# Folded attention: part of the output is stored in two unfinished parts, q's rotation reads the matmul banks, and the softmax scaling is one operation

## The chip, the core and the metric

The kernel runs on one core of one Trainium2 chip. A core has five engines that work side by side, each through its own queue and in the order of that queue: TensorE (PE in the profile; PEld is its weight load), VectorE (DVE), ScalarE (ACT), GpSimd (POOL) and SyncE (SP, which here issues most DMAs). They meet through semaphores. SBUF is the on-chip memory of 128 partitions, PSUM holds the matmul results in banks of 128 x 512 fp32, and HBM lies outside. The metric is the device time of one execution in microseconds (us); lower is better.

## What is computed

One layer of a hybrid decoder on x of 1024 x 1024 fp32: a norm, one projection into nine parts, retention (branch A), sliding-window attention with sinks (branch B), gates, and a SwiGLU feed-forward. The change touches branch B:

```python
aq = rotary(aq.reshape(B, S, ATTN_Q_HEADS, ATTN_HEAD_DIM), pos)   # 16 heads of 64
...
scores = jnp.einsum('bnqhgd,bnkhd->bnhgqk', qb, kb) * (d ** -0.5)
scores = jnp.where(mask, scores, -1e30)                           # window of 128
m = jnp.maximum(jnp.max(scores, axis=-1, keepdims=True), sink)
e = jnp.exp(scores - m)
probs = e / (jnp.sum(e, axis=-1, keepdims=True) + jnp.exp(sink - m))
out = jnp.einsum('bnhgqk,bnkhd->bnqhgd', probs, vb)
branch_b = ay.reshape(B, S, ATTN_Q) @ w_attn_out[l]
```

where rotary makes `x1*cos - x2*sin` and `x2*cos + x1*sin` from the two halves of a head.

## The kernel before

**Numbers in two parts.** Matmul operands are split into a high part (rounded to the matmul's format, called hi, `wh`, `ph`) and the rest (lo, `wl`, `pl`), and each product is three matmuls: hi x hi, hi x lo, lo x hi. ACT makes a high part (a cast), DVE the low part (a subtraction). `split` (L131) does this for weights; their tiles `wh` and `wl` have two buffers each.

**q, in quads.** `quad_q(g)` (L403) makes the rotated q of the four heads of group g. Its weights arrive as two raw slabs and are split into two pairs of tiles, one for the first halves of the heads (z = 0), one for the second (z = 1). Four groups of 24 matmuls follow, each into one of three banks tagged `acc`, in the order (z, half) = (0,0), (0,1), (1,0), (1,1), where half is a half of the 1024 positions. After each, ACT copies the bank out with the bias (L427). When both z of a half are there, DVE and ACT turn them (L437 to L446): four multiplications by cos and sin, a subtraction and an addition, and two splits. The result `stg` (one buffer, shared with k's staging) is stored to HBM as 1 MB (`q_d`, L448) and loaded back in another layout (L450).

**Attention, in 32 units.** A unit is one of four groups of heads (g) and one of eight blocks of 128 positions (b). `u_scores` (L462) makes the scores of four heads into two banks; ACT copies one part, DVE puts the masked other part in (L483) and takes the minimum (the scores are negated), with the sink in an extra column that POOL writes (L469); ACT makes the exponentials (L493), DVE the reciprocal of their sum, and ACT scales each of the four heads (L498). In block 0 one DVE operation per head (L490) masks and takes the minimum. A window of two blocks of keys is folded into one block of 128 columns, since of each pair of keys only one is inside the window. `u_transpose` (L500) turns the probabilities on TensorE (`pT`), splits them, and by a mask makes `qh`, `ql` for the difference of v's two blocks; `u_values` (L520) multiplies with v into one bank `pv`. In that bank two heads share each pair of quarters, and its rows of the two halves have to be added across: ACT copies them (L529, L530), DVE adds (L531, L532), ACT and DVE split the sum (L534, L535) into hi and lo, which overwrite q. After four blocks SP stores the result, 1 MB, to `ay_d` (L568).

**What sets the order.** quad_q(0) runs alone. Then a generator `Fill` supplies other matmuls between the pieces of the units: quad_q(1) to (3) and the gate projections `g6`, ... (`dense_g`, L178, in two groups of 24 each, evicted by ACT with a tanh). In a step i, TensorE's program has the transposes of unit i-1, the scores of unit i, some 7 to 8 steps of three fill matmuls, and the values of unit i-1 (L555 to L574). A scheduler then orders each engine's queue by priorities; weights are pulled ahead (`high_priority`). Half-way the v weights `wv` are loaded into a buffer that the q of groups 0 and 1 has left, and later pairwise subtracted (L578).

**The column pairs.** Ten pairs of column blocks (`w*`, from L783 on) of the projection follow, in seven products each (P1 to P7, Strassen's scheme), with operands split three products ahead by `wprep_to` (ACT hi, DVE lo, POOL the sums of weights). Here DVE, ACT and POOL work in the order in which the code is written (`in_order`, L903). Results of pairs 0, 2, 4 and 6 are rotated: r lies in a tile tagged `rr` (three buffers), SP copies its halves crosswise to `xw`, then POOL and DVE multiply (`turn`, L839) and DVE adds and SP stores to `rk_d` (`total`, L843), two and three products later. At pair 2 the attention output of groups 0 and 1 comes back into `ay` (`load_ay(0)`, L891), to be used after the column pairs; at the end of them that of groups 2 and 3.

## Time and profile before

| what | value |
|---|---|
| median of 3 runs | 1569.12 us (1568.94 to 1569.2) |
| the profiled execution: its time / its span | 1566.55 us / 1564.8 us |
| mean granted TensorE clock | 0.998 |
| attention stage, first q matmul to first v matmul | 42.1 to 351.0 us |
| v projection | 351 to 427 us |
| column pairs | 427 to 620 us |
| DMA traffic | 228.43 MB, 146 GB/s on the mean |

The profile is of one execution. A busy time is the sum of an engine's instructions; "idle before, <-releaser" is the time an engine stood still ahead of a group of instructions and what ended it; in the table of waits a row reads: engine, what waited, for whom, us in total, times, longest. Names like `aq`, `pT`, `stg` are tiles of the program, and L-numbers its lines. A matmul's record is longer (0.39 us) than the distance to the next one, since they overlap in the array; the pace is read from the starts. PEld rows are loads of weights for the next matmul and run beside the current one.

### The profile page before, as it was taken

The page shows a single profiled execution, that of the slowest core. Times are in us where ns is not written, and L with a number is a line of the kernel's source. Part 1 is how long each engine was busy: PE and PEld are TensorE (multiplying, and loading weights), DVE is VectorE, ACT ScalarE, POOL GpSimd, SP SyncE. Part 2 cuts the span into 40 slices and gives each one's busy share as a digit, 9 for nine tenths or more (in the row PEclk, how much of TensorE's full clock was granted, in tenths as well). Part 3 has the DMA queues.
Part 4 walks back from the last instruction along what each step waited for, and adds up shares of the span by engine and source line. Part 5 has one row for each costly group of instructions (what it writes and reads, how often), then busy time and mean ns, then how long its engine had stood idle before and what let it go on. Part 6 is the DMA issues. An engine that isn't in the chain of part 4 may idle for free.

```text
span 1564.8 us, 20561 instructions
## 1 busy us (share of the span) xinstructions
PE 1549.0 (99%) x7323; PEld 1284.4 (82%) x7323; DVE 1016.2 (65%) x1668; ACT 735.2 (47%) x1556; POOL 375.3 (24%) x320
## 2 busy tenths in 40 slices
PE   9999999999999999999999999999999999999998
PEld 8887777788888888888888888888888888888886
DVE  6559878677667663877557789444444444678756
ACT  6358878834233333544224366333333333444445
POOL 2000000000055441000021124655555555100001
PEclk9999999999999999999999999999999999999999
DMA  6554655340464455654565402333333333862233
GB/s 219 168 160 123 208 209 162 129 134 35 154 204 149 138 165 189 227 193 150 175 195 190 167 1 88 121 102 102 108 103 109 105 101 102 289 255 90 92 102 127
DMA packets 152581, 228.43 MB, mean 146 GB/s; under 512 B 9307, under 2 KB 81821, under 8 KB 150942
## 3 DMA queue, kind: packets, MB, share of 16 engines
q1 hardware_dynamic: 152476, 227.10, 44.4%
q8 instruction: 58, 0.95, 0.2%
q14 instruction: 45, 0.37, 0.1%
q10 hardware_dynamic: 2, 0.00, 0.0%
HBM read 152.36 MB, written 69.99 MB: 142 GB/s over the span
## 4 chain that ended last, share of the span: by engine, by line
PE 88%; ACT 6%; DVE 4%; issue 1%; DMA 1%; SPq 0%; POOL 0%; POOLq 0%; ACTq 0%; DVEq 0%
PE fA L1545 15%; PE fB L1545 8%; PE dA L1847 7%; PE wA L869 7%; PE dxP L1847 6%; PE fC L1545 4%; PE wB L869 3%; PE wo L1379 3%; PE va L714 3%; PE woP L1379 2%; PE vP L714 2%; PE acc_ba L161 2%; PE acc_ba L159 2%; PE acc_ba L160 2%; PE acc_bb L159 2%; PE acc_bb L160 2%
## 5 line engine op out<-in xcount | busy, mean ns | idle before, releaser
L1847 PE MATMUL dA<-dwP,daP 128*128 128x512 f32 x528 | 120.6, 389 | 0.0
L1847 PEld LDWEIGHTS dA<-dwP,daP 128*128 128x128 f32 x528 | 99.0, 188 | 20.7 <-DVE dwP L135 0.2
L1847 PE MATMUL dxP<-dwP,daP 128*128 128x512 f32 x396 | 90.2, 389 | 0.0
L1847 PEld LDWEIGHTS dxP<-dwP,daP 128*128 128x128 f32 x396 | 74.3, 188 | 15.4
L159 PE MATMUL acc_g<-h,wh_g 128*128 128x512 f32 x192 | 76.9, 401 | 0.6 <-ACT wh_g L132 0.6
L469 POOL COPY sc<-nsink 128x4 f32<-128x4 f32 x32 | 11.2, 349 | 273.6 <-PE pT L505 237.2
L160 PE MATMUL acc_g<-h,wh_g 128*128 128x512 f32 x192 | 76.4, 398 | 0.0
L161 PE MATMUL acc_g<-h,wl_g 128*128 128x512 f32 x192 | 76.4, 399 | 0.0
L1620 POOL TENSOR_TENSOR xf<-xf 128x512 f32<-128x512 f32 x40 | 61.6, 1541 | 30.4 <-issue 28.8
L1551 POOL TENSOR_TENSOR xf<-xf 128x512 f32<-128x512 f32 x33 | 47.3, 1435 | 58.5 <-ACT xf L1553 26.9
L493 ACT ACTIVATE sc<-sc,nm 128x129 f32<-128x129 f32 x128 | 50.4, 397 | 19.3 <-DVE nm L485 15.4
L135 DVE TENSOR_TENSOR dwP<-wd,dwP 128x512 fp32r<-128x512 f32 x77 | 52.7, 684 | 4.6 <-ACT dwP L132 4.6
L1752 POOL TENSOR_TENSOR rs_f<-tot,mhalf 128x1 f32<-128x1 f32 x8 | 4.8, 606 | 205.4 <-DVE tot L1749 205.4
L132 ACT CAST daP<-daP 128x512 fp32r<-128x512 f32 x42 | 26.0, 621 | 55.0 <-PE dxP L1847 26.7
L132 ACT CAST dwP<-wd 128x512 fp32r<-128x512 f32 x77 | 47.4, 616 | 8.8 <-PE dA L1847 6.6
L159 PE MATMUL acc_bb<-ay,wh_bb 128*128 128x512 f32 x128 | 51.2, 400 | 0.0
L160 PE MATMUL aq<-h,wh_aq 128*128 128x512 f32 x128 | 50.6, 395 | 0.0
L161 PE MATMUL aq<-h,wl_aq 128*128 128x512 f32 x128 | 50.5, 395 | 0.0
L159 PE MATMUL aq<-h,wh_aq 128*128 128x512 f32 x128 | 50.3, 393 | 0.0
L160 PE MATMUL acc_bb<-ay,wh_bb 128*128 128x512 f32 x128 | 50.3, 393 | 0.0
L161 PE MATMUL acc_bb<-ay,wl_bb 128*128 128x512 f32 x128 | 50.1, 391 | 0.0
L159 PE MATMUL acc_ba<-yg,wh_ba 128*128 128x512 f32 x128 | 49.9, 390 | 0.0
(840 smaller groups left out, 4350.1 us busy)
## 6 DMA issues: line engine op xcount, KB each, us to landing
act_d<-xf SPq DMA_DIRECT2D x77, 256.0 KB, 2.0
daP<-act_d SPq DMA_DIRECT2D x21, 512.0 KB, 3.5
q_d<-stg SPq DMA_DIRECT2D x8, 1024.0 KB
q<-q_d SPq DMA_DIRECT2D x32, 256.0 KB, 6.0
ay_d<-q SPq DMA_DIRECT2D x8, 1024.0 KB
ay<-ay_d SPq DMA_DIRECT2D x4, 2048.0 KB, 14.3
wr_daP<-act_d SPq DMA_DIRECT2D x14, 512.0 KB, 6.8
wr_g<-in_w_in SPq DMA_DIRECT2D x12, 512.0 KB, 4.2
```

What stands on the lines that cost most here:

```text
L132: nc.scalar.copy(hi, raw)
L135: return nc.vector.tensor_tensor(out=lo, in0=raw, in1=f32(hi), op=ALU.subtract)
L159: nc.tensor.matmul(pt, hi[:, k, :], xh, start=(k == 0), stop=False)
L160: nc.tensor.matmul(pt, hi[:, k, :], xl, start=False, stop=False)
L161: nc.tensor.matmul(pt, lo[:, k, :], xh, start=False, stop=(k == 7))
L493: nc.scalar.activation(sc[:, j, 0:P + 1], sc[:, j, 0:P + 1], AF.Exp, scale=-1.0, bias=nm[:, j:j + 1], accum_out=den[:, j:j + 1])
L714: nc.tensor.matmul(vbanks[pr][tt], x_[:, c], w[:, u, :], start=(fresh and k + z == 0), stop=(k == 3 and z == 2), skip_group_check=not fresh)
L869: nc.tensor.matmul(pt, o[:, w, k, :], v, start=(first and k + z == 0), stop=(k == 3 and z == 2), skip_group_check=not first)
L1379: nc.tensor.matmul(bank, v[:, q + u, k, c], w[y][:, k % 2, :], start=(first and z == 0), stop=(last and z == 2), skip_group_check=not tracked)
L1545: nc.tensor.matmul(pt, o[:, w, k, :], v, start=(first and n == 0), stop=(n == 11), skip_group_check=not first)
L1620: nc.gpsimd.tensor_tensor(out=o, in0=a, in1=b, op=op)
L1847: nc.tensor.matmul(banks[tt], a[:, u, c], w[:, v, :], start=(fresh and f + z == 0), stop=(f == NP - 1 and z == 2), skip_group_check=not fresh)
```

## The change

1. In groups 0 and 1, `u_values` no longer adds, splits and overwrites q: ACT copies the bank as it is to a tile `xy` (two buffers), and POOL issues a DMA of 256 KB per unit to a new HBM tile `xy_d`. The four stores to `ay_d` of these groups go. Groups 2 and 3 are as before.
2. `load_ay(0)` brings the two parts to the places of hi and lo in `ay` (eight DMAs of 512 KB). `split_ay`, called after product P3 of the pairs 4, 5, 6 and 7, adds the two, and makes hi (ACT) and lo (DVE), two halves each time, with a scratch tile `ays` from the tag `rr`.
3. `quad_q` runs its groups as (half, z) = (0,0), (0,1), (1,0), (1,1). ACT's copy with the bias goes; DVE multiplies straight from the bank, adding the bias in the same operation (`scalar_tensor_tensor`), twice per bank. The tiles `ra` and `rb` go, and k's and v's staging take the tags `ph`, `qh` and `ql`.
4. The scaling by the reciprocal is one DVE operation on four heads in groups 0 and 1, and on two heads in groups 2 and 3, where ACT still scales the other two.

```diff
...
     mb_d = dram.tile([8, P, S], F32, name="mb_d")
     ay_d = dram.tile([4, P, 4, S], F32, name="ay_d")
+    xy_d = dram.tile([2, P, 4, S], F32, name="xy_d")
     v_d = dram.tile([P, NB, D], F32, name="v_d")
     rk_d = dram.tile([8, P, S], F32, name="rk_d")
...
         def ak_evac(half, pt):
             c = slice(half * 512, half * 512 + 512)
-            xb = r512("ra", 2, f"kxb{half}")
+            xb = r512(("ph", "qh")[half], 1, f"kxb{half}")
             nc.scalar.activation(xb, pt, AF.Identity, bias=akb, scale=-0.125)
             stg = w1.tile([P, 4, 512], F32, tag="stg", bufs=1, name=f"kstg{half}")
...
 
         def av_evac(half, pt):
-            vt = r512("rb", 1, f"vt{half}")
+            vt = r512("ql", 1, f"vt{half}")
             nc.scalar.activation(vt, pt, AF.Identity, bias=bcol[:, 33:34], scale=1.0)
             p2 = ps("t", 2, f"vT{half}")
...
                     nc.vector.tensor_tensor(out=lo, in0=rv_[:, :, z], in1=f32(hi), op=ALU.subtract)
             hp.__exit__(None, None, None)
-            ab = {}
-            for z, half in ((0, 0), (0, 1), (1, 0), (1, 1)):
+            for half, z in ((0, 0), (0, 1), (1, 0), (1, 1)):
                 pt = acc(f"aq{g}{z}{half}")
                 yield from mm_g(pt, w[z], H, half * 512)
-                t = r512("ra" if z == 0 else "rb", 2 - z, f"q{g}{z}{half}")
-                nc.scalar.activation(t, pt, AF.Identity, bias=bcol[:, QB + 4 * z + g:QB + 4 * z + g + 1], scale=1.0)
-                ab[z, half] = t
+                c = slice(half * 512, half * 512 + 512)
+                if z == 0:
+                    stg = w1.tile([P, 4, 512], F32, tag="stg", bufs=1, name=f"stg{g}{half}")
+                    s0, s1, s2, s3 = (stg[:, i, :] for i in range(4))
+                bias = bcol[:, QB + 4 * z + g:QB + 4 * z + g + 1]
+                for o, tab in (((s2, 0), (s0, 1)), ((s1, 1), (s3, 0)))[z]:
+                    nc.vector.scalar_tensor_tensor(out=o, in0=pt, scalar=bias, in1=atab[:, tab, c], op0=ALU.add,
+                                                   op1=ALU.mult)
                 if z == 0:
                     yield
                     continue
-                c = slice(half * 512, half * 512 + 512)
-                a, b = ab[0, half], t
-                stg = w1.tile([P, 4, 512], F32, tag="stg", bufs=1, name=f"stg{g}{half}")
-                s0, s1, s2, s3 = (stg[:, i, :] for i in range(4))
-                cos, sin = atab[:, 0, c], atab[:, 1, c]
-                nc.vector.tensor_tensor(out=s2, in0=a, in1=cos, op=ALU.mult)
-                nc.vector.tensor_tensor(out=s1, in0=b, in1=sin, op=ALU.mult)
                 nc.vector.tensor_tensor(out=s2, in0=s2, in1=s1, op=ALU.subtract)
-                nc.vector.tensor_tensor(out=s0, in0=a, in1=sin, op=ALU.mult)
-                nc.vector.tensor_tensor(out=s3, in0=b, in1=cos, op=ALU.mult)
                 nc.vector.tensor_tensor(out=s3, in0=s3, in1=s0, op=ALU.add)
                 nc.scalar.activation(s0.bitcast(F32R), s2, AF.Copy)
...
             rd = tiny.tile([P, 4], F32, tag="rd", name=f"rd{g}{b}")
             nc.vector.reciprocal(rd, den)
-            for j in range(4):
+            nd = 4 if g < 2 else 2
+            nc.vector.tensor_tensor(out=sc[:, 0:nd, 0:P], in0=sc[:, 0:nd, 0:P],
+                                    in1=rd[:, 0:nd].rearrange("p (j o) -> p j o", o=1).to_broadcast([P, nd, P]),
+                                    op=ALU.mult)
+            for j in range(nd, 4):
                 nc.scalar.activation(sc[:, j, 0:P], sc[:, j, 0:P], AF.Copy, scale=rd[:, j:j + 1])
 
...
                 for z, p in enumerate(hl):
                     nc.tensor.matmul(pv, vb[:, g // 2, :], p, start=(n + z == 0), stop=(n == len(parts) - 1 and z == 1))
+            if g < 2:
+                t = w1.tile([P, 512], F32, tag="xy", bufs=2, name=f"xy{g}{b}")
+                nc.scalar.copy(t, pv)
+                nc.gpsimd.dma_start(xy_d[g, :, :, qc], t.rearrange("p (j q) -> p j q", j=4))
+                return
             pvv = pv.rearrange("p (i z q) -> p i z q", i=2, z=2)
             tm = w1.tile([P, 2, P], F32, tag="tm", bufs=1, name=f"tm{g}{b}")
...
                     g, b, _, Bt, jb, _ = geo(i - 1)
                     c = slice((b // 4) * 512, (b // 4) * 512 + 512)
-                    nc.sync.dma_start(ay_d[g, :, :, c], f32(Bt[:, jb:jb + 4, c]))
+                    if g > 1:
+                        nc.sync.dma_start(ay_d[g, :, :, c], f32(Bt[:, jb:jb + 4, c]))
             if i == 2 * NB + 4:
                 wv = act.tile([P, 16, 512], F32, tag="B", name="wv")
...
         AY.append(act.tile([P, 8, 1024], F32R, tag="B", name=f"ay{z}"))
         for g in range(2):
-            nc.sync.dma_start(f32(AY[z][:, 4 * g:4 * g + 4, :]), ay_d[2 * z + g])
+            if z:
+                nc.sync.dma_start(f32(AY[z][:, 4 * g:4 * g + 4, :]), ay_d[2 * z + g])
+                continue
+            for r in range(2):
+                for u in range(2):
+                    nc.sync.dma_start(f32(AY[z][r * 64:r * 64 + 64, 4 * g + u:4 * g + u + 3:2, :]),
+                                      xy_d[g, u * 64:u * 64 + 64, r:r + 3:2, :])
+
+    def split_ay(k):
+        for q in range(2):
+            c = slice(q * 512, q * 512 + 512)
+            hi, lo = AY[0][:, 2 * k, c], AY[0][:, 2 * k + 1, c]
+            t = wtile("rr", 3, f"ays{k}{q}")
+            nc.vector.tensor_tensor(out=t, in0=f32(hi), in1=f32(lo), op=ALU.add)
+            nc.scalar.copy(hi, t)
+            nc.vector.tensor_tensor(out=lo, in0=t, in1=f32(hi), op=ALU.subtract)
 
     qTs, kTs, kts, rgs = {}, {}, {}, {}
...
             if (j, pr) == (2, "P1"):
                 load_ay(0)
+            elif j in (4, 5, 6, 7) and pr == "P3":
+                split_ay(j - 4)
             elif (j, pr) == (8, "P5"):
                 load_kq(0, 0)
```

How this moves instructions, at three places. Lines after L63 are shifted by 1 to 23 in the changed kernel.

First, DVE's queue in the first quad. `stg_739` is the rotation of quad 0's first half, `q_683` and `q_737` the copies of its two banks, `wl_aq_799` and `wl_aq_801` the low parts of quad 1's weights (z = 0 and z = 1). Before:

```order
L420 TENSOR_TENSOR wl_aq_799<-wr_aq_802,wh_aq_798 128x512
L336 TENSOR_TENSOR kstg_607<-kxb_605,kstg_607 128x512
L420 TENSOR_TENSOR wl_aq_799<-wr_aq_808,wh_aq_798 128x512
L437 TENSOR_TENSOR stg_739<-q_683,atab 128x512
L438 TENSOR_TENSOR stg_739<-q_737,atab 128x512
L440 TENSOR_TENSOR stg_739<-q_683,atab 128x512
L439 TENSOR_TENSOR stg_739<-stg_739 128x512
L441 TENSOR_TENSOR stg_739<-q_737,atab 128x512
L442 TENSOR_TENSOR stg_739<-stg_739 128x512
```

In the changed kernel the rotation is `stg_684`, the banks are `aq_659` and `aq_687` (quad 0's first and second group), and quad 1's weights for z = 0 are `wl_aq_792` with the high part `wh_aq_791`:

```order
L337 TENSOR_TENSOR kstg_608<-kxb_606,kstg_608 128x512
L421 TENSOR_TENSOR wl_aq_792<-wr_aq_795,wh_aq_791 128x512
L421 TENSOR_TENSOR wl_aq_792<-wr_aq_801,wh_aq_791 128x512
L432 SCALAR_TENSOR_TENSOR stg_684<-aq_659,bcol,atab 128x512 x2
L432 SCALAR_TENSOR_TENSOR stg_684<-aq_687,bcol,atab 128x512 x2
L437 TENSOR_TENSOR stg_684<-stg_684 128x512
L438 TENSOR_TENSOR stg_684<-stg_684 128x512
```

The first operations that read a bank stand behind quad 1's weight subtractions, whose buffer (that of quad 0's z = 0 weights) is read until the third group. The fourth group writes the bank of `aq_659` again.

Second, TensorE's queue at quad 1's end, where `s_890` and `s_899` are the scores of unit 0, `s_946` and `s_956` those of unit 1, and `aq_873` and `aq_926` quad 1's third and fourth group. Before, all four groups of quad 1 and two of the gate's stood ahead of the scores:

```order
L161 MATMUL acc_g_1_1163<-h_111,wl_g_1024 128x512
L159 MATMUL acc_g_1_1163<-h_111,wh_g_1023 128x512
L477 MATMUL s_885<-kst,q_641 128x128 [waits DMAHW5_49,DMAHW6_49,DMAHW4_49,DMAHW7_49,DMAHW2_49,DMAHW0_49]
L478 MATMUL s_885<-kst,q_641 128x128
L477 MATMUL s_885<-kst,q_641 128x128
```

After, the scores come between the third and the fourth group, which waits for DVE:

```order
L162 MATMUL aq_873<-h_112,wl_aq_792 128x512
L473 MATMUL s_890<-kst,q_642 128x128 [waits DMAHW5_49,DMAHW6_49,DMAHW4_49,DMAHW7_49,DMAHW2_49,DMAHW0_49]
...
L473 MATMUL s_946<-kst,q_642 128x256 [waits DVE_49]
L474 MATMUL s_946<-kst,q_642 128x256
L473 MATMUL s_946<-kst,q_642 128x256
L474 MATMUL s_946<-kst,q_642 128x256
L473 MATMUL s_956<-kst,q_642 128x256 [waits DVE_49]
L474 MATMUL s_956<-kst,q_642 128x256
L473 MATMUL s_956<-kst,q_642 128x256
L474 MATMUL s_956<-kst,q_642 128x256
L160 MATMUL aq_926<-h_111,wh_aq_793 128x512 [waits DVE_49]
```

and in DVE's queue the reads of `aq_807`, the bank that `aq_926` writes, stand behind the gate's weights and unit 0's four minima (`nm_888`):

```order
L136 TENSOR_TENSOR wl_g_1003<-wr_g_1000,wh_g_1002 128x1024
L486 ISA sc_886,nm_888<-s_890,amask,nsink 128x128
L486 ISA nm_888 128x1
L486 ISA sc_886,nm_888<-s_890,amask,nsink 128x128
L486 ISA nm_888 128x1
L486 ISA sc_886,nm_888<-s_899,amask,nsink 128x128
L486 ISA nm_888 128x1
L486 ISA sc_886,nm_888<-s_899,amask,nsink 128x128
L486 ISA nm_888 128x1
L432 SCALAR_TENSOR_TENSOR stg_832<-aq_807,bcol,atab 128x512 x2
```

Third, DVE's queue in the column pairs, after product P3 of pair 4. `r_5020` and `r_4863` are the same result before and after, `w5P_5098` and `w5P_4949` the weights of product P5 of pair 5. Before:

```order
L834 SCALAR_TENSOR_TENSOR r_5091<-wB_4988,bcol,u_4983 128x512
L844 TENSOR_TENSOR r_5020<-r_5020,xw_5022 128x512
L135 TENSOR_TENSOR w5P_5098<-wr_wp_4886,w5P_5098 128x512
L849 TENSOR_TENSOR r_5114<-wC_5101,p_5047 128x512
L841 TENSOR_TENSOR r_5069<-r_5069,rtabkT 128x512
```

After (the waits are printed with the rows):

```order
L840 SCALAR_TENSOR_TENSOR r_4934<-wB_4831,bcol,u_4826 128x512 [waits DMAHW0_49,DVE_49,PE_49]
L850 TENSOR_TENSOR r_4863<-r_4863,xw_4865 128x512 [waits DVE_49,Pool_49]
L913 TENSOR_TENSOR ays_4941<-ay_4440 128x512 [waits DMAHW6_49,DVE_49]
L915 TENSOR_TENSOR ay_4440<-ays_4941,ay_4440 128x512 [waits Activation_49]
L913 TENSOR_TENSOR ays_4945<-ay_4440 128x512 [waits DVE_49]
L915 TENSOR_TENSOR ay_4440<-ays_4945,ay_4440 128x512 [waits Activation_49]
L136 TENSOR_TENSOR w5P_4949<-wr_wp_4729,w5P_4949 128x512 [waits Activation_49]
L855 TENSOR_TENSOR r_4965<-wC_4952,p_4890 128x512 [waits DMAHW1_49,PE_49]
```

On ACT the two copies L914 stand in the same way ahead of the high part of `w5P_4949`. After P3 of pair 6 the rows are the same with pair 7's weights.

## The prediction

> **What bounds the kernel now.** I read the busy times first, then the chain that ended last, then the busy time by stage.

> ```profile
> PE 1549.0 (99%) x7323; PEld 1284.4 (82%) x7323; DVE 1016.2 (65%) x1668; ACT 735.2 (47%) x1556; POOL 375.3 (24%) x320
> PE 88%; ACT 6%; DVE 4%; issue 1%; DMA 1%; SPq 0%; POOL 0%; POOLq 0%; ACTq 0%; DVEq 0%
> 106.00:142.00 36.00, 35.87 (x186) 28.65 (x184) 32.30 (x74) 32.45 (x110) 2.80 (x6) 1.00 0.64 187
> 427.00:620.00 193.00, 192.62 (x853) 158.84 (x852) 114.90 (x133) 74.67 (x127) 81.35 (x56) 1.00 0.52 168
> ```

> TensorE is the bound: 88% of the chain is PE. Both kernels issue the same matmuls, so only the time in which PE waits can change. In the rows of stages the columns are the stretch, its length, the busy us of PE, weight loads, DVE, ACT and POOL, the clock, the DMA share and GB/s. In the attention stage ACT and DVE are at 32 of 36 us, as loaded as they get; in the column pairs DVE has 78 us free, ACT 118, and PE loses 0.4 us. So the attention stage has something to win and the column pairs have only something to lose.

> How much can be won? The stage runs from the first q matmul to the first v matmul.

> ```profile
> 42.11 0.40 PE L159 MATMUL aq<-h,wh_aq 128*128 128x512 f32 x1
> ...
> 57.23 0.39 PE L160 MATMUL aq<-h,wh_aq 128*128 128x512 f32 x1
> ...
> 59.95 0.39 PE L160 MATMUL aq<-h,wh_aq 128*128 128x512 f32 x1
> ...
> 95.37 0.28 PE L478 MATMUL s<-kst,q 128*128 128x128 f32 x1
> 95.48 0.27 PE L477 MATMUL s<-kst,q 128*128 128x128 f32 x1
> ...
> 96.82 0.28 PE L478 MATMUL s<-kst,q 128*128 128x256 f32 x1
> 96.94 0.28 PE L477 MATMUL s<-kst,q 128*128 128x256 f32 x1
> ...
> 350.99 0.62 PE L714 MATMUL va<-vP,h 128*128 128x512 f32 x2
> ```

> Starts follow each other at 0.2267 us for 512 columns (2.72 us for 12), 0.11 for 128, 0.12 for 256. The stage has 40 groups of 24 (16 of q, 24 of the gates) and 120 value matmuls of 512 columns: 1080 x 0.2267 = 244.8 us. The scores add 32 x 0.11 + 224 x 0.12 = 30.4, the transposes 128 x 0.11 = 14.1: 289.3 us. It takes 308.9, so 19.6 us are lost. The waits name the losers (us, times, longest):

> ```profile
> PE pT L505 <- ACT sc L498: 2.1, 4, 1.2
> PE pv L526 <- DVE tm L532: 1.7, 3, 0.8
> PEld pT L505 <- ACT sc L498: 9.8, 31, 1.6
> PEld pv L526 <- ACT ph L507: 3.0, 6, 0.9
> PEld pv L526 <- DVE qh L515: 2.8, 6, 0.9
> ```

> These five make 19.4, but a late weight load is partly covered by the matmul in flight, and some of the 19.6 is slower turning between kinds of matmul. I take **15 us of real waits**, an estimate, of which about 11 hang on L498, the scaling.

> **The change part by part.** *Scaling, output copy and store.*

> ```profile
> 98.59 1.28 ACT L498 ACTIVATE sc<-sc,rd 128x128 f32<-128x128 f32 x4
> L135 DVE TENSOR_TENSOR dwP<-wd,dwP 128x512 fp32r<-128x512 f32 x77 | 52.7, 684 | 4.6 <-ACT dwP L132 4.6
> L534 ACT CAST q<-tm 128x256 fp32r<-128x256 f32 x32 | 12.8, 400 | 1.2 <-DVE tm L532 1.2
> L529 ACT COPY tm<-pv 64x256 f32<-64x256 f32 x32 | 11.8, 370 | 4.5 <-PE pv L526 3.8
> L531 DVE TENSOR_TENSOR tm<-pv,tm 64x256 f32<-64x256 f32 x32 | 13.3, 415 | 25.9 <-ACT tm L530 25.8
> L507 ACT CAST ph<-pT 128x512 fp32r<-128x512 f32 x32 | 18.6, 583 | 0.9 <-PE pT L505 0.5
> ```

> For groups 0 and 1 four scalings on ACT (1.28 us) become one on DVE, 128x512 with two inputs: 0.68. For groups 2 and 3 two stay (0.64) beside a 256-column one on DVE (0.42, as L531). So the chain scores, copy, mask, minimum, exponentials, reciprocal, scaling shortens by 0.6 us per unit. In 16 units ACT also loses two half copies and a cast (0.37 + 0.37 + 0.40) for one 128x512 copy from a bank (0.58, as L507): with the scaling ACT saves 1.8 us per unit there. DVE loses three operations of 0.42 and gains 0.68, and no longer idles on ACT in between (L531's 25.9). 31 late loads on L498 average 0.3 us, less than the 0.6 saved, so I let 11 fall to 2.5 and the other waits of about 4 to 3: **5.5 us of 15 stay, a gain of 9.5** (bounds 6, where the DVE queue takes back half of the 0.6, and 12, where all of L498 goes).

> *Rotation from the banks.* The nearest rows to its new operation, one of the same kind in the column pairs and what follows it on DVE:

> ```profile
> 525.99 0.75 DVE L834 SCALAR_TENSOR_TENSOR r<-wB,bcol,u 128x512 f32<-128x512 f32 x1
> 526.66 0.68 DVE L844 TENSOR_TENSOR r<-r,xw 128x512 f32<-128x512 f32 x1
> ```

> In each of the 8 rotations four multiplications of 0.68 become four of 0.75 that read a bank, and ACT loses 16 copies of 0.69 in all. What changes is when a bank comes free: before, ACT copied it out at once; now two DVE operations behind everything in DVE's queue do. The three `acc` banks turn, so every fourth group waits for DVE. And the new order of the groups frees z = 0's weight buffers one group later. Before, at the corresponding turn of weights:

> ```profile
> 59.05 0.39 PE L159 MATMUL aq<-h,wh_aq 128*128 128x512 f32 x1
> ...
> 53.62 0.62 ACT L419 CAST wh_aq<-wr_aq 128x512 fp32r<-128x512 f32 x1 [4.21 <-PE aq L160]
> ...
> 54.28 0.69 DVE L420 TENSOR_TENSOR wl_aq<-wr_aq,wh_aq 128x512 fp32r<-128x512 f32 x1 [4.14 <-ACT wh_aq L419]
> ...
> 86.22 1.05 ACT L132 CAST wh_g<-wr_g 128x1024 fp32r<-128x1024 f32 x1 [3.44 <-PE aq L160]
> ...
> 87.31 1.22 DVE L135 TENSOR_TENSOR wl_g<-wr_g,wh_g 128x1024 fp32r<-128x1024 f32 x1 [3.72 <-ACT wh_g L132]
> ...
> 95.91 0.35 DVE L490 CUSTOM_DVE_ANT_0 sc<-s,amask,nsink 128x128 f32<-128x128 f32 x1 [7.38 <-PE s L478]
> ...
> 97.00 0.68 DVE L437 TENSOR_TENSOR stg<-q,atab 128x512 f32<-128x512 f32 x1
> ```

> Quad 0: the cast waits for the end of the third group (now), as it waited at 53.62 for the end of the second. The fourth group would start at 59.05. In DVE's queue quad 1's two weight subtractions stand ahead of the bank reads: cast 0.66 (53.62 to 54.28), two subtractions at about 0.65 (0.69, overlapping at the ends), two reads of the first bank at 0.67 (525.99 to 526.66): 0.66 + 1.3 + 1.34 = 3.3 us after 59.0. **PE waits 3.2 us**, where it had no wait (bounds 2.9 to 3.6).
> Quad 1: the fourth group stands behind unit 0's and unit 1's scores, and its bank is read behind the gate's weights (cast 1.09 after the seventh group's end, subtraction 1.2) and the four masked minima of unit 0 (97.00 - 95.91 = 1.09): 1.09 + 1.2 + 1.09 + 1.34 = 4.7, against 8 x 0.11 + 8 x 0.12 = 1.8 of score matmuls. **2.8 us** (2.5 to 3.0). The one buffer `stg` also hangs on q's store:

> ```profile
> 73.45 0.69 DVE L437 TENSOR_TENSOR stg<-q,atab 128x512 f32<-128x512 f32 x1 [5.42 <-DMA q_d<-stg]
> ```

> 5.4 us from the end of a rotation to its store's landing. Quad 0's first store then lands at about 71.5 and the bank for the sixth group is free at 72.8, 0.3 us before that group is due; I count nothing, but 1 us if it is 1 us late.

> *The output's way back.* The four 1 MB stores of groups 0 and 1 become 16 of 256 KB from POOL, each ahead of the sink copy of the unit after next.

> ```profile
> L469 POOL COPY sc<-nsink 128x4 f32<-128x4 f32 x32 | 11.2, 349 | 273.6 <-PE pT L505 237.2
> ...
> 528.04 0.53 SPq L845 DMA_DIRECT2D rk_d<-r  x1
> ```

> POOL has at least 1.4 us there (transposes 0.44 and scores 0.96 stand between). No row shows a DMA issued by POOL; the nearest are this copy (0.35) and SP's issue of a store (0.53). I take 0.5, which stays hidden. [...]

> *The column pairs.* Four times 2 x (add, ACT copy, subtract) go in, DVE +10 us, ACT +5, both with room; the output's load, now in eight pieces, is issued two pairs (some 38 of the 193 us) ahead of its first use and costs nothing. But the operations stand in a written order:

> ```profile
> 527.26 1.79 DVE L135 TENSOR_TENSOR w5P<-wr_wp,w5P 128x512 fp32r<-128x512 f32 x1
> ...
> 531.23 2.88 PE L869 MATMUL wB<-h,w5P 128*128 128x512 f32 x12
> ...
> DMA to landing us min/median/max: 3.1/3.6/4.2
> ```

> At pair 4 the scratch tile `ays` is the `rr` buffer of the r whose total, the row of 526.66, ended at 527.34, so the add waits until that r's store (issued 528.04, landing row of L845) is in: 528.04 + 3.1 = 531.1 at the least. Then, in order: add 0.68, copy 0.66, subtract and add 1.3, copy 0.66, subtract 0.6, and only then the low half of the weights of product P5 of pair 5, 0.68: 531.1 + 4.6 = 535.7. Before, that low half was made at 527.26. PE needs it with the third matmul of the product due at 531.23, at 531.7. **PE waits about 4.0 us**; pair 6 has the same rows, so 8.0 in all (3.0 each if the second half overlaps more, 5.2 with the longest landing). Pairs 5 and 7 have no r in `rr` ahead: there the 4.6 us start some 0.9 us after product P3 (one 0.68 addition and the hand-off) and the low half is due 5.9 us after it (two products of 2.72, two matmuls): 0.4 us to spare, nothing counted.
> [...]

> *The v weights* load 2 x 512 KB earlier and are subtracted ahead of unit 17's scaling; the load lands at about the time DVE arrives: 0, at most 2 us.

> **Sum.** -9.5 + 3.2 + 2.8 + 8.0 = **+4.5 us** on the profiled execution of 1566.55 us (span 1564.8): 1571.05. The median of the runs is 1569.12, 2.6 higher, so **1573.6**. Its own range: -12 + 2.9 + 2.5 + 6.0 = -0.6, and -6 + 3.6 + 3.0 + 10.4 + 2 = +13 at the most; both ends at once are unlikely, so 1569.5 to 1579.

> **Rivals.**
> *The gain shows and the column pairs hide their work* (faster). If the scratch tile doesn't wait for the store, because the buffer taken is another or the store is in before 528, add follows total at 527.3, the low half is ready at 527.34 + 4.6 = 531.9, and PE loses 0.2 us at each place. It decides at a landing of about 527.4. Then -9.5 + 6.0 + 0.4 = -3.1: 1566.0, and with the gain at its bound of 12, 1563.5. For it: DVE has 78 us free there. Against it: the wait on a DMA stands in the add's row, and L845 never lands under 3.1 us.
> *Gain and losses cancel* (same). Gain 12, column places at 3.0: -12 + 6.0 + 6.0 = 0: 1569.1. For it: L498 is named in 31 of 32 units.
> *POOL is late* (slower still). Should a DMA's 512 pieces hold POOL for more than 1.4 us, the sink copy and with it each minimum is late: at 2.1 us, 0.7 x 16 = 11 us more, 1585. The low POOL load (2.8 of 36 us) speaks against; no row shows the price.
> *ACT wasn't what PE waited for*: DVE, at 32.3 of 36, gets the scaling; then the gain is 3: -3 + 14 = +11, 1580.

> **How the numbers follow.** My forecast (slower, 1573.6) 0.45, POOL late or DVE the new limit 0.10, cancelled 0.25, hidden 0.20. Bound of what can be told from no change: 0.2%, 3.1 us, so 1566.0 to 1572.3. The forecast's lower edge falls in "same", the hidden case's upper edge too: slower 0.50, same 0.28, faster 0.22. The range of 1564 to 1580 leaves out the end of the hidden case and most of the late POOL.

> **What would show it.** PE idle at L160 of `aq`, released by DVE `stg`, of 3 us in quad 0 and 2.5 to 3 in quad 1; the waits of `pT` on scaling down from 11.9 to under 4 us, with DVE's L494 named in place of ACT; `wB` of pairs 5 and 7 starting 4 us late with DVE's add L913 waiting for `rk_d`. I am wrong if `ays` never waits for a DMA, if the fourth q groups start on time, or if DVE's queue makes `pT` or `pv` wait as long as before.

## The result and the profile after

The changed kernel takes **1583.41 us** (median of four runs, 1582.62 to 1584.12); the kernel before takes 1569.03 beside it. The ratio is **1.0093, interval 1.0078 to 1.0108**: slower by 14.4 us, where +4.5 was forecast. The profiled execution took 1582.78 us, with a span of 1581.0.

The page after, busy times and chain:

```profile
PE 1553.5 (98%) x7323; PEld 1291.0 (82%) x7323; DVE 1023.2 (65%) x1668; ACT 694.9 (44%) x1420; POOL 383.9 (24%) x336
PE 87%; DVE 5%; ACT 3%; issue 2%; DMA 1%; POOL 1%; SPq 0%; POOLq 0%; DVEq 0%; ACTq 0%
```

ACT's work fell by 40 us and TensorE is still the bound. But PE is busy 4.5 us *longer* (1549.0 before) with the same 7323 matmuls: some of them ran slower. Next the busy time by stage, before and then after: attention, v projection, column pairs (columns: stretch, length, busy us of PE, weight loads, DVE, ACT, POOL, granted clock, DMA share, GB/s).

```profile
42.11:350.98 308.87, 302.23 (x1470) 244.31 (x1469) 229.21 (x482) 213.03 (x657) 10.98 (x31) 1.00 0.52 162
350.98:427.19 76.21, 76.21 (x337) 63.01 (x336) 53.97 (x74) 26.14 (x38) 1.08 (x1) 1.00 0.23 80
427.19:618.56 191.37, 190.99 (x841) 157.34 (x840) 113.54 (x132) 74.67 (x127) 81.16 (x56) 1.00 0.52 166
```

```profile
44.60:352.44 307.84, 299.44 (x1471) 247.75 (x1470) 229.83 (x466) 168.05 (x513) 18.58 (x47) 0.99 0.51 162
352.44:428.65 76.21, 76.21 (x338) 63.02 (x337) 54.04 (x74) 26.09 (x38) 1.12 (x1) 1.00 0.22 73
428.65:634.09 205.44, 196.15 (x842) 159.08 (x841) 121.51 (x147) 79.20 (x135) 81.57 (x56) 0.98 0.51 157
64.83:68.24 3.41, 3.41 (x8) 2.73 (x9) 2.66 (x5) 0.87 (x2) 0.00 (x0) 0.52 0.00 0
538.47:542.43 3.96, 3.89 (x10) 2.77 (x10) 3.26 (x7) 2.57 (x5) 0.00 (x0) 0.59 0.17 66
```

The attention stage became 1.0 us shorter, not 3.5 (-9.5 + 3.2 + 2.8); the column pairs 14.1 longer, not 8.0. The last two rows show the new thing: directly behind a wait the granted clock is 0.52 and 0.59. The clock's record has four such stretches of half clock (granted clock 0.50), each 3.413 us long, beginning at 64.7, 92.0, 539.2 and 583.5; the kernel before has none from its first q matmul on, until the program's last 5 us. The first q matmul starts some 2.5 us later in the changed kernel than before; it varies between 42.1 and 44.6 in all executions below, so I compare lengths of stages.

PE's longest waits over the whole program, after (what waited, for whom, us in total, times, longest):

```profile
PE wB L875 <- ACT w7P L133: 3.9, 1, 3.9
PE wB L875 <- ACT w5P L133: 3.6, 1, 3.6
PE aq L160 <- DVE stg L432: 3.5, 2, 3.2
PE s L473 <- DVE nm L486: 1.9, 1, 1.9
PE pT L505 <- DVE sc L494: 1.5, 3, 1.0
PE wA L875 <- DVE w2P L136: 1.2, 2, 0.9
```

Before, no single wait of PE exceeded 1.2 us in these stages. Quad 0's turn in the timeline after (start, duration, and in brackets the idle time before and who ended it):

```profile
61.27 0.39 PE L162 MATMUL aq<-h,wl_aq 128*128 128x512 f32 x1
...
64.83 0.79 PE L160 MATMUL aq<-h,wh_aq 128*128 128x512 f32 x1 [3.17 <-DVE stg L432]
65.42 0.63 PE L161 MATMUL aq<-h,wh_aq 128*128 128x512 f32 x1
65.84 0.63 PE L162 MATMUL aq<-h,wl_aq 128*128 128x512 f32 x1
```

TensorE stands for 3.17 us ahead of the fourth group, where 3.2 was forecast, and then its matmuls follow each other at 0.42 us instead of 0.2267. Pair 4 and the start of pair 5's product P5, after:

```profile
530.12 0.68 DVE L850 TENSOR_TENSOR r<-r,xw 128x512 f32<-128x512 f32 x1
...
533.94 1.21 DVE L913 TENSOR_TENSOR ays<-ay 128x512 f32<-128x512 f32 x1 [3.13 <-DMA rk_d<-r]
...
537.80 0.61 ACT L133 CAST w5P<-wr_wp 128x512 fp32r<-128x512 f32 x1
538.54 0.69 DVE L136 TENSOR_TENSOR w5P<-wr_wp,w5P 128x512 fp32r<-128x512 f32 x1
...
538.47 4.90 PE L875 MATMUL wB<-h,w5P 128*128 128x512 f32 x12 [3.62 <-ACT w5P L133]
```

The add waits 3.13 us for r's store, which SP issued at 531.46, and the weights' split stands behind it. Twelve matmuls take 4.90 us here, 2.88 before: 2.0 us on top of the 3.6 of idle time.

The difference, put together from these traces (us):

| place | forecast | idle time | half clock | sum |
|---|---|---|---|---|
| attention stage without the quads' turns | -9.5 | -10.2 | | -10.2 |
| quad 0's turn | +3.2 | 3.3 | 1.7 | +5.0 |
| quad 1's turn | +2.8 | 2.7 | 1.5 | +4.2 |
| pairs 5 and 7 | +8.0 | 7.9 | 4.1 | +12.0 |
| pairs 2 and 3 | 0 | 2.1 | | +2.1 |
| after the column pairs, to the last matmul | 0 | 0.5 | | +0.5 |
| sum | +4.5 | 6.3 | 7.3 | +13.6 |

The first row's -10.2 is what is left of the stage's -1.0 once the turns are taken out. Each half clock is the length of the stretch less what its matmuls need at 0.2267 us. The two profiled executions are 16.2 us apart: 13.6, the later start of 2.5, and 0.2 behind the last matmul. The medians differ by 14.4.

### The profile page after: what moved, and what is told of

The parts are those of the page before. It is cut to its first block, busy times and chain, and to the rows that moved or that the text cites. A ratio compares the mean times of both kernels' runs of the same rounds, so it can differ in the third digit from the quotient of the medians.

```text
span 1581.0 us, 20464 instructions
## 1 busy us (share of the span) xinstructions
PE 1553.5 (98%) x7323; PEld 1291.0 (82%) x7323; DVE 1023.2 (65%) x1668; ACT 694.9 (44%) x1420; POOL 383.9 (24%) x336
## 4 chain that ended last, share of the span: by engine, by line
PE 87%; DVE 5%; ACT 3%; issue 2%; DMA 1%; POOL 1%; SPq 0%; POOLq 0%; DVEq 0%; ACTq 0%
PE fA L1568 15%; PE fB L1568 8%; PE dA L1870 7%; PE dxP L1870 6%; PE wA L875 5%; PE fC L1568 4%; PE wB L875 3%; PE wo L1402 3%; PE va L720 3%; PE acc_g L160 2%; PE acc_g L161 2%; PE acc_g L162 2%; PE woP L1402 2%; PE vP L720 2%; PE acc_ba L160 2%; PE acc_ba L162 2%
## 5 line engine op out<-in xcount | busy, mean ns | idle before, releaser
L160 PE MATMUL acc_g<-h,wh_g 128*128 128x512 f32 x192 | 75.5, 393 | 0.0
L465 POOL COPY sc<-nsink 128x4 f32<-128x4 f32 x32 | 7.4, 233 | 213.9 <-PE pT L505 168.7
L160 PE MATMUL aq<-h,wh_aq 128*128 128x512 f32 x128 | 51.6, 403 | 3.5 <-DVE stg L432 3.5
L1775 POOL TENSOR_TENSOR rs_f<-tot,mhalf 128x1 f32<-128x1 f32 x8 | 4.8, 606 | 205.4 <-DVE tot L1772 205.4
L589 POOL TENSOR_TENSOR wr_wp<-wr_wp 128x512 f32<-128x512 f32 x10 | 16.2, 1616 | 154.0 <-DVE w0P L136 121.5
L160 PE MATMUL acc_bb<-ay,wh_bb 128*128 128x512 f32 x128 | 50.9, 399 | 0.0
```

The lines of the kernel that those rows point to most:

```text
L160: nc.tensor.matmul(pt, hi[:, k, :], xh, start=(k == 0), stop=False)
```

## The experiments

Twelve kernels were run. Lengths are of each run's profiled execution; the last column lists where stretches of half clock begin, from the first q matmul to the program's last 5 us. They are 3.413 us long, but 6.827 in e1 at 64.1, in e2 at 582.0 and all four times in e7, and 10.240 in e9.

| run | median us | ratio to before, 95% | attention | column pairs | half clock from |
|---|---|---|---|---|---|
| before | 1569.03 | | 308.9 | 191.4 | none |
| after | 1583.41 | 1.0093 (1.0078 to 1.0108) | 307.8 | 205.4 | 64.7, 92.0, 539.2, 583.5 |
| e1 | 1576.06 | 1.0052 (1.0037 to 1.0067) | 310.2 | 199.0 | 64.1, 94.8 |
| e2 | 1585.16 | 1.0105 (1.0085 to 1.0126) | 311.0 | 205.8 | 131.5, 541.1, 582.0 |
| e3 | 1577.28 | 1.0067 (1.0051 to 1.0082) | 314.1 | 200.0 | 133.4, 191.5, 543.0 |
| e4 | 1566.86 | 0.9995 (0.9986 to 1.0005) | 308.8 | 191.4 | 161.7 |
| e5 | 1571.42 | 1.0021 (1.0010 to 1.0031) | 307.3 | 195.4 | 64.3, 91.6 |
| e6 | 1563.82 | 0.9970 (0.9959 to 0.9982) | 300.9 | 194.1 | none |
| e7 | 1604.33 | single run | | 226.3 | 538.3, 586.1, 613.4, 640.7 |
| e8 | 1574.90 | 1.0037 (1.0023 to 1.0051) | 316.1 | 191.2 | 63.7, 91.0, 275.3 |
| e9 | 1574.82 | 1.0045 (1.0032 to 1.0058) | 301.1 | 205.9 | 509.4 |
| e10 | 1579.41 | 1.0075 (1.0060 to 1.0091) | 308.2 | 202.2 | 64.7, 92.0 |
| e11 | 1566.04 | 0.9989 (0.9980 to 0.9998) | 303.5 | 197.4 | none |
| e12 | 1564.23 | 0.9976 (0.9967 to 0.9985) | 301.0 | 196.0 | none |

### e1: the scratch tile from another tag

The changed kernel, with `ays` in a buffer of `xw`, so that it waits for no store.

```diff
-            t = wtile("rr", 3, f"ays{k}{q}")
+            t = wtile("xw", 3, f"ays{k}{q}")
```

> The changed kernel, with the scratch tile of split_ay taken from the tag xw (whose last buffer DVE itself has just read) in place of rr, so that no store has to land first. Theory A (each of the two waits in the column pairs is the store's landing, 3.8 us of idle TensorE, and then one window of 3.4 us at half clock, 2.0 us more): wB of pairs 5 and 7 starts at most 0.5 us late, no half-clock window after 430 us, 11 to 12 us less than the changed kernel: 1571.5 to 1572.5. Theory B (DVE, ACT and their written order are crowded there, whatever the scratch): at most 4 us less, 1579 or more. Theory C (the half-clock windows there do not come from the idle time): the waits go, the windows stay, 7 to 8 us less, 1575 to 1576.

The column pairs fell by 6.5 us, and their two half-clock stretches went; the time lies between what A and B gave. The attention stage, in which nothing was changed, is 2.4 us longer than in the changed kernel, 1.3 of it because the half clock at 64.1 lasts twice as long. But the places still cost 2.7 us each instead of nearly nothing (the distance from pair 5's first product to pair 6's is 21.7 us, 24.9 after, 19.0 before). DVE in e1:

```profile
533.17 1.67 DVE L913 TENSOR_TENSOR ays<-ay 128x512 f32<-128x512 f32 x1
...
536.24 1.66 DVE L913 TENSOR_TENSOR ays<-ay 128x512 f32<-128x512 f32 x1
...
539.13 3.14 PE L875 MATMUL wB<-h,w5P 128*128 128x512 f32 x11 [1.94 <-ACT w5P L133]
```

The add was priced at 0.68 and takes 1.67, while POOL multiplies `xw` at the same moment (L846 from 532.87 to 534.29 and from 535.63 to 537.35). So the store makes 6.6 of the 12.0 us lost at these places, half clocks included, and the written order, twice add, copy, subtract ahead of the weights, the other 5.4. The 1.9 us of idle time brought no half clock here.

### e2 and e3: the rotation as before

The changed kernel with part 3 taken back; since the space is short, `xy` shares the buffers of the gates' tanh tiles. e3 has e1's edit as well.

```diff
-            for half, z in ((0, 0), (0, 1), (1, 0), (1, 1)):
+            for z, half in ((0, 0), (0, 1), (1, 0), (1, 1)):
...
-                t = w1.tile([P, 512], F32, tag="xy", bufs=2, name=f"xy{g}{b}")
+                t = gt.tile([P, 512], F32, tag="st", bufs=2, name=f"xy{g}{b}")
```

> The changed kernel, with the rotation and the order of the four q groups as before (ACT copies the banks out), all else as changed; the xy tiles share a tag with the gates' tanh tiles to make room. Theory A: the waits of quad 0 (3.3 us) and quad 1 (2.7 us) and their two half-clock windows (1.7 and 1.4 us) go, against at most 1 us for ACT's copies: 8 to 9 us less, 1574.5 to 1575.5. Theory D (the rotation from the banks is what frees ACT, and the attention stage wins through it): the units wait again as before, and no more than 3 us are left: 1580 or more.

> The changed kernel with both edits (scratch from xw, rotation as before): only the scaling, the output copy and the split in the column pairs are left of the change. Theory A: -11.5 - 8.5 from 1583.4: 1563.4, 5.6 us under the kernel before (ratio 0.9964). Rival: the savings overlap (a wait that only moves), 1567 or more. The product P7 of pair 2 starts some 2 us late as in the changed kernel, if the eight loads of the output are what delays it.

Both quads' waits are gone and the stage is not shorter but 3.2 us longer than in the changed kernel (e3, with the same code there: 6.2; a wait of 2.10 us with the half clock at 191.5 is in it). Part of that comes from the shared tag: a tanh tile waits for the store of `xy`, and PE behind it. ACT and PE in e2:

```profile
131.17 0.69 ACT L551 ACTIVATE tb<-acc_g,bhalf 128x512 f32<-128x512 f32 x1 [3.58 <-DMA xy_d<-xy]
...
131.91 0.80 PE L160 MATMUL aq<-h,wh_aq 128*128 128x512 f32 x1 [2.94 <-ACT tb L551]
```

With its half clock this is 4.6 us, so the stage would be some 306.4 without it (worked out, not run). The quads' 9.2 us therefore seem to have bought something: with the rotation reading the banks, ACT is rid of 16 copies, and without that PE waits for ACT's `ph` and `xy` (2.6 us in e2, 0.7 after). e2 can't price the rotation cleanly; e6 does it better.

### e4: scaling alone

The kernel before with part 4 only.

```diff
-            for j in range(4):
+            nd = 4 if g < 2 else 2
+            nc.vector.tensor_tensor(out=sc[:, 0:nd, 0:P], in0=sc[:, 0:nd, 0:P],
+                                    in1=rd[:, 0:nd].rearrange("p (j o) -> p j o", o=1).to_broadcast([P, nd, P]),
+                                    op=ALU.mult)
+            for j in range(nd, 4):
```

> The kernel before with the scaling alone changed (one DVE operation for four heads, or for two). If the waits on the scaling are most of what the change wins, as the prediction has it: the waits of pT on L498 fall from 11.9 to under 5 us and the time to 1562 to 1565. Rival: DVE, which still has the three operations on the output in groups 0 and 1, becomes the bound there: pT and pv wait for DVE instead, 1567 to 1571.

No change that can be measured. The waits that it was meant for fell (`pT` on scaling, weight loads included, from 11.9 to 5.1 us), others came. PE in e4:

```profile
PE aq L161 <- DVE wl_aq L420: 1.5, 1, 1.5
PE pT L509 <- DVE sc L498: 1.1, 2, 0.9
PE acc_g L159 <- ACT wh_g L132: 0.8, 1, 0.8
PEld pT L509 <- DVE sc L498: 2.3, 3, 1.3
PEld pT L509 <- ACT sc L502: 1.7, 7, 0.5
```

Three of these idles (0.90, 0.75 and 0.47 us) end within 3 us of each other, and a half-clock stretch follows at 161.7. DVE has 245.6 us to do in this stage, against 229.2 before, and the split of the weights comes late instead.

### e8: the rotation alone

The kernel before with part 3 only: new order of the groups, DVE reading the banks, other tags for k's and v's staging.

```diff
-            for z, half in ((0, 0), (0, 1), (1, 0), (1, 1)):
+            for half, z in ((0, 0), (0, 1), (1, 0), (1, 1)):
```

> The kernel before with the rotation from the banks and the new order of the groups alone. Theory A: quad 0's wait of 3.3 us and quad 1's of 2.7 us with their half-clock windows stand as in the changed kernel (9 us together), and the units gain up to 3 us by ACT's 16 copies that go: attention stage 314 to 318 us, the whole 1574 to 1578. Rival (the waits come from the whole change, through a different order of the queues): less than 4 us slower than before.

The stage is 7.3 us longer, and the quads' waits are there as in the changed kernel:

```profile
PE aq L159 <- DVE stg L431: 3.8, 2, 3.2
PE s L472 <- DVE nm L485: 1.9, 1, 1.9
```

They cost 9.5 us with their half clocks; a third stretch at 275.3 follows four short idles within 4 us (0.43, 0.16, 0.39, 0.90), so the rest of the stage is some 2 us shorter, or 4 with that stretch taken out. So part 3 alone brings the loss in the quads.

### e5: the column work spread out

The changed kernel with e1's scratch tile, and the adds, the copies and the subtractions of each `split_ay` each put behind a product of their own instead of all behind P3.

```diff
-            elif j in (4, 5, 6, 7) and pr == "P3":
-                split_ay(j - 4)
+            elif j in (4, 6) and pr == "P3":
+                for n in range(2):
+                    wlater.extend((i + 3 + 2 * n + m, f) for m, f in enumerate(split_ay(j - 4 + n)))
```

> The changed kernel, with split_ay's three steps (two additions, two copies, two subtractions) put at three successive products instead of one, three to seven products after P3 of the pairs 4 and 6, and the scratch from the tag xw. e1_scratch_xw still lost 2.4 us at each place, where DVE's additions ran beside POOL at 1.7 us each and DVE and ACT passed the tile back and forth four times ahead of the next weights. Theory A (it is this chain in the written order, not the amount of work, that delays the weights): both places cost nothing, the column pairs take 193.5 us (191.4 and pair 2's 2.1), the whole 1571 to 1572. Theory B (DVE is short of time there): 196 us or more, 1574 or more.

The distances at pairs 5 and 7 are 19.04 us again, as before: the loss of 12.0 there was order and scratch, not work. The column pairs still take 4.0 us more than before: 2.3 at pairs 2 and 3, and 1.0 and 0.8 at pairs 6 and 8.

### e6: quads and column work mended

e5, with `load_ay(0)` written twelve products later (at pair 3's P5), and on DVE the next quad's weight subtractions put behind the bank reads, as well as the gate's behind quad 1's.

```diff
-                    nc.vector.tensor_tensor(out=lo, in0=rv_[:, :, z], in1=f32(hi), op=ALU.subtract)
+                    behind(nc.vector.tensor_tensor(out=lo, in0=rv_[:, :, z], in1=f32(hi), op=ALU.subtract), g - 1)
...
+            d = split(raw, hi, lo)
+            if name == "g6":
+                behind(d, 1)
...
-            if (j, pr) == (2, "P1"):
+            if (j, pr) == (3, "P5"):
```

> As e5_split_staggered, with the output's load moved from pair 2 to pair 3 (P5), and with the reads of quad 0's and quad 1's first two banks ordered ahead of the next weights' subtractions in DVE's queue. Theory A: pair 2's 2.1 us go (column pairs 191.4 to 191.6), quad 0's wait of 3.3 us goes and quad 1's falls to about 1 us, and with them all half-clock windows: attention stage 300 to 301.5 us, the whole 1561.5 to 1563.5, ratio 0.9955 to 0.997. Rival (the waits only move to the next group or unit): attention stage 304 us or more, 1565 or more. If the eight loads are not what delays pair 2, its 2.1 us stay.

**Faster than both kernels**, 0.3% under the one before: 0.9970 (0.9959 to 0.9982). The profiled execution is the fastest of six (1561.42). The attention stage is 300.9 us, 8.0 less than before; e9 and e12, with the same code there, took 301.1 and 301.0. PE in that stage of e6:

```profile
PE pT L517 <- DVE sc L506: 1.8, 4, 1.1
PE aq L170 <- DVE stg L442: 1.0, 2, 0.6
PE s L485 <- DVE nm L498: 0.3, 1, 0.3
```

The turns wait 1.3 us in all instead of 5.4, and no half clock is left. The column pairs keep +2.7 over before. The edit to `load_ay(0)` moved nothing: SP's queue is not in the order of the code, and the eight loads go out as early in e6 as in the changed kernel, from 9.3 us ahead of the first column product to 29.3 us behind it (first row the changed kernel, second e6; min/median/max ns of an issue, first and last start):

```profile
L905 SPq DMA_DIRECT2D ay<-xy_d x8: 524/600/1313, 419.3 to 457.9; - x8
L917 SPq DMA_DIRECT2D ay<-xy_d x8: 524/600/2092, 410.1 to 448.7; - x8
```

So e6 tests the quads and the column work, and says nothing on where the output is loaded.

### e7: waits of chosen size

The kernel before, with dummy multiplications on DVE, whose result is not used, ahead of the weights of pairs 4 to 9: 8, 8, 10, 10, 12, 12 of them. The output is still computed in full.

```diff
+            if pr == "P3" and 3 <= j <= 8:
+                t = wtile("xw", 3, f"dose{j}")
+                for _ in range((8, 8, 10, 10, 12, 12)[j - 3]):
+                    nc.vector.tensor_tensor(out=t, in0=rtab[0][:, 0:512], in1=rtab[0][:, 0:512], op=ALU.mult)
```

> The kernel before, with 8, 8, 10, 10, 12 and 12 idle multiplications put into DVE's queue after product P3 of the column pairs 3 to 8, ahead of the low half of the weights of the product after next: TensorE then waits for some 0 to 4 us, six times, in a stage where it runs without a break otherwise. Theory A (a wait above some 2 to 3 us costs, beside itself, one 3.4 us window at half clock, 1.7 us): the long ones are each followed by a window of clock 0.5 and matmul starts 0.43 us apart, the short ones (under 1.2 us) by none. Theory C (the windows have another cause than idle time): no window, or windows that do not follow the waits.

PE's waits in the column pairs of e7, and then what followed the wait for pair 6 (`w6P`) and that for pair 5 (`w5P`):

```profile
PE wB L869 <- DVE w7P L135: 6.7, 1, 6.7
PE wB L869 <- ACT w9P L132: 6.5, 1, 6.5
PE wB L869 <- DVE w5P L135: 5.3, 1, 5.3
PE wB L869 <- DVE w8P L135: 4.1, 1, 4.1
PE wB L869 <- DVE w6P L135: 1.2, 1, 1.2
```

```profile
562.00:566.00 4.00, 2.76 (x11) 1.84 (x12) 3.93 (x7) 1.06 (x3) 0.00 (x0) 1.00 0.00 0
...
540.30:546.00 5.70, 5.70 (x15) 4.53 (x16) 5.00 (x8) 2.75 (x5) 1.27 (x1) 0.58 0.42 123
```

The wait of 1.2 us leaves the clock at 1.00; the four of 4.1 to 6.7 us each bring half clock, for 6.83 us this time. Part of it falls into the wait itself, so it costs 1.7 to 2.8 us beside the idle time. The changed kernel's waits come from other work than this; the clock falls all the same.

### e10: TensorE kept busy during the wait

The changed kernel with 16 more matmuls ahead of P5 of pairs 5 and 7, whose result isn't read; the output is computed in full.

```diff
+        if j in (5, 7) and pr == "P5":
+            idle = ps("pv", 1, f"idle{j}")
+            for _ in range(16):
+                nc.tensor.matmul(idle, H[0][:, 0, 0:P], HX["P1"][0][0], start=True, stop=True)
```

> The changed kernel, with 16 matmuls of 512 columns whose results nobody reads (3.6 us) ahead of product P5 of the pairs 5 and 7, where TensorE waits 3.8 and 4.1 us. The weights come no earlier. Theory A (idle time is what brings the half-clock windows): the same lateness of P5, no window after 430 us, and 3.5 to 4 us less than the changed kernel, 1579.5 to 1580. Theory C (something else in that place lowers the clock): the windows stay, the same time as the changed kernel, 1583 to 1584.

Both places in e10:

```profile
533.00:545.00 12.00, 12.00 (x53) 9.44 (x52) 9.75 (x13) 5.11 (x9) 2.81 (x3) 1.00 0.30 87
575.00:590.00 15.00, 13.41 (x58) 10.33 (x57) 10.48 (x14) 5.69 (x10) 4.66 (x4) 1.00 0.49 165
```

The clock stays at 1.00 although the weights come no earlier, and with 32 matmuls *more* the column pairs are 3.2 us shorter than in the changed kernel (of the whole time the ratios' intervals overlap). So it is TensorE's idle time that takes the clock down, not what delays the weights. The gain at the two places is 1.3 and 0.8 us, though, not the 2 that each half clock cost. By the starts of its matmuls, P5 began 3.8 and 4.8 us late here (3.8 and 4.1 after). In pair 5, two matmuls recorded as unread ones ran in the midst of P5, and in both pairs its first matmuls stood 0.34 to 0.47 us apart: 0.7 and 0.6 us more. Why pair 7's weights came 0.8 us later wasn't settled; the rest of the 3.2 is at pairs 2 and 3, where nothing was changed.

### e11: the mended kernel with scaling on ACT

e6 with part 4 taken back.

```diff
-            nd = 4 if g < 2 else 2
...
-            for j in range(nd, 4):
+            for j in range(4):
```

> As e6_all_mended, with the scaling back on ACT, four operations, as before the change. e4_scaling_alone gained nothing alone, since DVE made weights late in its stead. If the scaling still carries the gain of the attention stage once the output's and the rotation's work is off the units, as the prediction has it: the waits of pT on L498 come back, attention stage 304 to 307 us against 300.9, the whole 3 to 6 us over e6. Rival (the output copy and the rotation carry it): attention stage under 302.5.

The old wait returns (weight loads of `pT` in e11):

```profile
PEld pT L513 <- ACT sc L506: 10.6, 31, 1.2
```

and the stage takes 303.5 us, 2.5 more than e6. That lies between the two expectations. In the mended kernel the scaling thus brings 2.5 of the stage's 8.0, and rotation and output together, measured against before, the other 5.4. The column pairs of e11, whose code is e6's, took 197.4 us, 3.3 more, of which 2.3 are at pairs 2 and 3: in that stage one execution can't tell differences of 1 or 2 us.

### e9 and e12: where the output is loaded

The remaining loss at pairs 2 and 3: DVE waits longer for the crosswise copies of r (the kernel before, then the changed one):

```profile
479.06 0.69 DVE L841 TENSOR_TENSOR r<-r,rtabkT 128x512 f32<-128x512 f32 x1 [2.91 <-DMA xw<-r]
```

```profile
481.77 1.83 DVE L847 TENSOR_TENSOR r<-r,rtabkT 128x512 f32<-128x512 f32 x1 [4.01 <-DMA xw<-r]
```

Suspected were the eight loads of 512 KB. e9 is e6 with all eight held in SP's queue behind the last store of pair 2 (they go out 70 us behind the first column product); e12 issues them one per product, written four at pair 3 and four at pair 5, each behind the last store of a result (they go out at 70 to 79 and at 108 to 118 us).

```diff
-                nc.sync.dma_start(rk_d[ct, :, c], r)
+                stored[0] = nc.sync.dma_start(rk_d[ct, :, c], r)
...
+                    tc.add_manual_dep(d.ins, stored[0].ins.name,
+                                      mybir.DependencyInfo(mybir.DependencyClass.NoSync, mybir.DependencyReason.DATA),
+                                      reason="after_pair")
```

> As e6_all_mended, with the eight loads of the output held in SP's queue behind the last store of pair 2 (in e6 the code came later, but SP's queue still had the loads in pair 1, as soon as their buffer was free). e6 still lost 1.7 us in pair 2, TensorE waiting for weights that DVE made late, after the crosswise copies xw of pair 2's first result had landed late. Theory E (the loads' 4 MB slow the copies xw): the 1.7 us go, column pairs 192.3 to 192.6, the whole 1.5 us under e6. Rival F (the loads have nothing to do with it): the 1.7 us stay, the column pairs take 194 again.

> As e6_all_mended, with the output's eight loads issued one at a time, one to a product, four in pair 3 and four in pair 5, each held in SP's queue behind the latest store; e9, with all eight together behind pair 2's last store, had that pair's following stores land 14 us late and cost 10.5 us. Theory E (a row of 4 MB in the queues delays whatever small transfer comes behind it): pair 2 waits no longer than before the change (0.7 us) and the stores of pairs 3 and 5 land in time: column pairs 192.5 to 193.5 us, the whole 0.5 to 1.5 us under e6. Rival: one load of 512 KB is enough to make a following copy or store late: 194.5 us or more.

In e9 pairs 2 and 3 lose 0.4 us against before, where e6 loses 1.0, the changed kernel 2.1 and e11, with e6's code, 3.3. The eight loads themselves hardly stand in the way of these copies: in the changed kernel the last is issued at 457.9, those whose landing is recorded land 6.8 to 7.8 us behind their issue, and the copies are issued at 476.6. But two other loads moved with them. Where the eight go out early, SP issues the loads of `rmask` and `rv` 42 to 46 us behind the first column product, right ahead of these copies (48 us); in the kernel before, e4, e7, e8, e9 and e12 they go out at 3 to 12 us. With `rmask` at 43.3 us pairs 2 and 3 lose 2.1 to 3.3 us (the changed kernel, e1, e2, e3, e5, e11), at 42.2 0.9 to 1.0 (e6, e10), and early at most 0.9. No run moves these two loads alone, so this is likely and not shown.

But behind the eight loads a gate's store is held up. SP's queue, DVE and PE in e9:

```profile
490.33 5.91 SPq L918 DMA_DIRECT2D ay<-xy_d  x8
...
514.12 0.69 DVE L868 TENSOR_TENSOR r<-wB,u 128x512 f32<-128x512 f32 x1 [14.48 <-DMA rg_d<-r]
...
516.18 4.62 PE L888 MATMUL wB<-h,w4P 128*128 128x512 f32 x12 [10.34 <-ACT w4P L141]
```

PE stands for 10.3 us and gets half clock on top. e12 has no such wait, and loses 0.9 at pairs 2 and 3 and 3.8 at pairs 6 to 8, more than e6 there (1.7). Its time can't be told from e6's, so spreading the loads is no gain over e6. That a store behind eight loads in a row lands late is shown; how much of the 2.7 us that e6 still loses in the column pairs the loads cause stays open.

## Why the prediction was wrong

**What bounds the kernel** was read rightly: TensorE, with the attention stage to win in and the column pairs to lose in. The time went to the places that it named.

**The step that failed** is "so only the time in which PE waits can change", and with it "PE waits 3.2 us", "2.8 us" and "about 4.0 us", each put into the sum as the wait alone. The idle times were right: 3.3, 2.7 and, for the two places in the column pairs, 7.9 us. But behind each of the four waits TensorE ran at half clock for 3.4 us, which cost 7.3 us in all; no term of the sum stood for that. e7 shows that waits made by other work bring it too, e10 that it doesn't come when the wait is filled. With it left out, the same trace gives +6.3 instead of +4.5; with it, +13.6. A second, smaller step failed too, the output's load put at nothing (below).

**Scaling, output copy and store.** The gain, forecast at 9.5, was 10.2 in the changed kernel and 8.0 in e6 with the turns' last 1.3 us of waits in it. The size was right partly by luck, since the reason was not: "about 11 hang on L498" made the scaling the main thing, and it is worth nothing measurable alone (e4) and 2.5 in company (e11). The waits of `pT` on the scaling fell from 11.9 to 6.2 us, not to 2.5, and all waits of `pT` together only to 10.7 (matmuls and weight loads added up). It was the waits of `pv` that went, from 12.4 to 1.1; they stay gone with the scaling back on ACT (1.7 in e11), and the rotation alone takes them to 4.3 (e8). How the 5.4 us of rotation and output divide no run shows. The rival that DVE would become the new limit came true in e4 and not in the whole change: there DVE's work in the stage stays as it was (229.2 and 229.8 us) and ACT's falls from 213.0 to 168.1.

**Quad 1.** The 2.8 us came as 2.7, but most of it at another place than forecast: 1.87 us ahead of unit 1's scores, which wait for unit 0's minima on DVE, and 0.35 ahead of the fourth group.

**POOL is late** fell: its 16 DMAs took 0.71 us each on the median and 0.92 at most (0.5 was taken), and nothing waits for the sink copy. They landed after 2.7 to 6.3 us, 4.8 on the median; no wait of PE is put down to them.

**The column pairs.** The waits of 3.8 and 4.1 us, forecast at 4.0, are partly luck, since two terms were off against each other. The store was taken at 3.1 us at the least, which makes the add wait 3.8 (531.1 less 527.34); the adds started 2.48 and 2.65 us behind the store's issue and had waited 3.13 and 3.00. So the row of 3.1 to 4.2, from which the 3.1 was taken, did not hold for these two stores. The first add in turn took 1.21 and 1.33 us beside POOL, not 0.68. The rival "the column pairs hide their work" held that with another buffer PE loses 0.2 us at each place; e1 had that buffer and lost 2.7. e5 shows that they do hide it when the work is spread out as well.

**The output's load**, "costs nothing", went with a loss of 2.1 us at pairs 2 and 3. It is also not issued "two pairs" ahead of its use: the call stands at pair 2, but SP issues the loads from 419.3 to 457.9, ahead of pair 2 and more than 70 us ahead of the first add, and SP's other loads change places with them. With the loads held back (e9) the loss is 0.4, but a larger one comes later; that the loads as such cause it is not shown.

**Pairs 5 and 7 hanging on nothing, and the v weights at 0**, held: pairs 6 and 8, whose weights stand behind the work put in there, take 19.04 and 19.07 us (19.04 before), and the v projection 76.21 in both.

## What to carry to other kernels

In these runs each wait of TensorE of 2.9 us or more cost 1.5 to 3.0 us beyond itself, so a change that trades many waits of 0.3 us for a few of 3 gains less than the idle time says: in the attention stage 4.2 us less of it became 1.0 us. Count the single waits and their spacing, not only their sum. When an engine works in written order, inserted work belongs in pieces behind several products, in scratch that no store in flight still holds. A load whose first use is far away can still delay the small transfers that stand behind it in its queue (in e9 a 256 KB store was waited for 14.5 us); where a load goes out is read from the queue of the engine that issues it, not from its place in the code (e6).
